# Layer 0 of a two-layer encoder: the dilated heads' queries and keys are projected together for the first four blocks of x, with the loads in that order

## Chip, core and metric

The kernel runs on one core of a Trainium2 chip, in one launch. The metric is the time of one execution on the device in microseconds (us); several runs give a median. One more execution was recorded by the hardware profiler.

The engines are named as in the profile: PE is TensorE, with PEld for the loads of its stationary operand, DVE is VectorE, ACT is ScalarE, POOL is GpSimd and SP is SyncE, which issues most of the loads.

## What is computed

Two layers of an encoder over 256 positions of width 1024, in float32. Each layer has a mixer with three kinds of attention heads, and then a gated feed-forward part with a short convolution. The change is in the first products of the first mixer: `h @ w_in_l`, whose columns hold nine parts, among them `qd` and `kd`, the queries and keys of the six dilated heads, 384 columns each and side by side.

```python
def mixer_sublayer(x, n1, w_in_l, qg, kg, rpb_l, og, w_out_l, tables):
    h = rms_norm(x, n1)
    proj = h @ w_in_l
    sizes = (NA_W, NA_W, NA_W, DIL_W, DIL_W, DIL_W, GQ_W, GKV_W, GKV_W)
    qa, ka, va, qd, kd, vd, qc, kc, vc = jnp.split(proj, cuts, axis=-1)
    ...
    qd = partial_rotary(rms_norm(heads(qd, H_DIL), qg[1]), cos1, sin1)
    kd = partial_rotary(rms_norm(heads(kd, H_DIL), kg[1]), cos1, sin1)
    out_d = dilated_window_attention(qd, kd, heads(vd, H_DIL), dil_idx, dil_val)
    ...
    return x + mix @ w_out_l
```

## The kernel before

**Numbers and products.** Every float32 operand of a product is split into a rounded part (`hi`, a cast on ScalarE) and the rest (`lo`, a subtraction on VectorE), and a product is made of three: hi x hi, hi x lo, lo x hi (`mm3`). x stands in SBUF as two tiles of 128 positions (t = 0, 1). For the products it is turned on TensorE, block by block: 1024 columns are eight blocks of 128 (k = 0 to 7). A block takes two transpositions, then ScalarE scales it by the gains of the norm into `hT_hi` and VectorE makes `hT_lo`. The gains themselves are loaded as rows and turned first (`gains_T`); the division by the root of the mean square comes later, in the heads.

**Units.** The weights come in units of up to 2048 columns per partition, `PROJ` for `w_in`: the first unit is dq (the dilated queries) with blocks 0 to 3, the second dq with blocks 4 to 7, the third and fourth dk in the same way, then dv, cq, ckv, aqk, av. A unit is loaded into one of four `raw` buffers (`load`), split in slices into one of two pairs `hi`, `lo` (`split`), and used (`unit`). In `projections` a unit's products go over t, then over its blocks, so a block of dq with 384 columns is six products: three for each t. Each of dq and dk needs two of the four PSUM banks `psa`; dv takes the banks of dq again, when their values have been scaled and copied out.

**Order.** The kernel is first written down as a list (`Plan.add`), and then ordered by the planner in `Plan.order`, which takes, over all engines, the operation that can start first by its own estimates, and of several the one with the lower rank. A rank is the place in the list, a shift (`later`) and a correction from the table `PLACES`, by number of the operation. `START` is the hand-written order of the first loads, on SP's queue and on ScalarE's, and `LANDS` the times at which the planner expects them. `WARM` products of a constant, 256 columns in bfloat16, run on TensorE before its first data are there; `WARM_MORE` of them fill gaps among the first transpositions.

Almost every operation has the line 520 in the profile (519 after the change), since one helper records them all; so rows are told apart by the names of tiles: `psa` and `psw` are PSUM banks of products and of the rest, `act_hT` the turned x, `wp_raw`, `wp_hi`, `wp_lo` the weights, `const_x` the input, `act_s2k` a work buffer that holds the gains' rows at first.

## Time and profile before

| | us |
|---|---|
| median of 3 runs | 595.01 |
| lowest and highest | 594.70, 595.23 |
| the profiled execution | 595.39 |
| its span, first to last instruction | 593.6 |
| PE busy in the span | 587.5 |
| DVE, ACT busy | 470.2, 412.1 |

A busy TensorE is not the same as one that waits for nothing: products are pipelined, and two that follow each other at once overlap in the rows. So holes are read from the starts of products, and from the waits of the weight loads (PEld), which the trace gives with what ended them.

### The profile page before, as it was taken

How to read it: one execution, taken by the hardware profiler on the slowest of the kernel's cores; microseconds unless marked ns; L12 is line 12 of the kernel's file. 1: busy time of each engine (PE TensorE's matmuls, PEld its weight loads, DVE VectorE, ACT ScalarE, POOL GpSimd, SP SyncE). 2: the span in 40 equal slices, each digit the busy share in tenths (PEclk: the TensorE clock that was granted, in tenths of full speed). 3: DMA queues.
4: the chain of work that ended last, by engine and by line, in shares of the span. 5: the costliest groups of instructions: out<-in, count | busy, mean ns of one | idle time of the engine just before them, and what ended most of it. 6: DMA issues, size and time to landing. Idle time of an engine off the chain costs nothing.

```text
span 593.6 us, 9687 instructions
## 1 busy us (share of the span) xinstructions
PE 587.5 (99%) x3424; PEld 506.9 (85%) x3424; DVE 470.2 (79%) x983; ACT 412.1 (69%) x1035; POOL 78.3 (13%) x126
## 2 busy tenths in 40 slices
PE   9999999999999999999999999999999999999997
PEld 7998887888888888888899988778888888888886
DVE  5799889888779879778787896777876867776596
ACT  7789988676575766756697998476665656564581
POOL 1734121250000000000032225321000000000000
PEclk9999999999999999999999999999999999999999
DMA  8892313565589599899556527943455735666411
GB/s 294 307 323 105 107 36 121 202 213 192 180 245 371 207 342 346 290 318 323 170 153 213 203 73 252 340 142 120 155 201 167 240 118 186 213 215 211 142 71 72
DMA packets 85073, 121.38 MB, mean 204 GB/s; under 512 B 9864, under 2 KB 69736, under 8 KB 85024
## 3 DMA queue, kind: packets, MB, share of 16 engines
q1 hardware_dynamic: 82752, 112.10, 56.5%
q0 software_dynamic: 1728, 8.39, 4.0%
q8 instruction: 27, 0.44, 0.3%
q10 hardware_dynamic: 544, 0.26, 0.1%
q14 instruction: 22, 0.18, 0.1%
HBM read 110.86 MB, written 9.88 MB: 203 GB/s over the span
## 4 chain that ended last, share of the span: by engine, by line
PE 90%; POOL 3%; issue 2%; DMA 2%; DVE 2%; ACT 0%; POOLq 0%; ACTq 0%
PE psw_w L520 50%; PE psa_a L520 40%; POOL small_rstd L520 1%; DMA wp_hi<-dram_khi 1%; POOL small_ms L520 1%; DMA wp_raw<-in_w_in_dram 1%; DVE act_z L520 0%; DVE wp_lo L520 0%; DVE act_s2k L520 0%; POOL act_scq L520 0%; ACT act_s2k L520 0%; DVE act_sw L520 0%; POOL act_sck L520 0%; POOL act_sqm L520 0%; POOL wp_lo L520 0%
## 5 line engine op out<-in xcount | busy, mean ns | idle before, releaser
L520 DVE TENSOR_TENSOR wp_lo<-wp_raw,wp_hi 128x512 fp32r<-128x512 f32 (+2 forms) x332 | 233.7, 733 | 36.6 <-ACT wp_hi L520 22.7
L520 ACT CAST wp_hi<-wp_raw 128x512 fp32r<-128x512 f32 (+2 forms) x332 | 202.4, 665 | 19.9 <-PE psa_a L520 10.1
L520 PE MATMUL psw_w<-act_hT,wp_hi 128*128 128x512 f32 x704 | 177.1, 392 | 0.0
L520 PEld LDWEIGHTS psw_w<-act_hT,wp_hi 128*128 128x128 f32 x704 | 129.0, 188 | 24.8 <-DVE act_hT L520 0.3
L520 PE MATMUL psa_a<-wp_hi,act_hT 128*128 128x384 f32 (+2 forms) x448 | 112.8, 333 | 0.1
L520 PEld LDWEIGHTS psw_w<-act_hT,wp_lo 128*128 128x128 f32 x704 | 94.8, 188 | 6.3
L520 PE MATMUL psw_w<-act_hT,wp_lo 128*128 128x256 f32 x704 | 99.0, 280 | 0.0
L520 PEld LDWEIGHTS psa_a<-wp_hi,act_hT 128*128 128x128 f32 x448 | 77.7, 188 | 3.2 <-ACT act_hT L520 0.3
L520 PE MATMUL psa_a<-wp_lo,act_hT 128*128 128x384 f32 (+2 forms) x224 | 72.8, 331 | 0.5 <-DVE wp_lo L520 0.4
L520 DVE TENSOR_TENSOR act_s2k<-psw_w,act_s2k 128x256 f32<-128x256 f32 x88 | 36.2, 421 | 40.0 <-ACT act_s2k L520 39.6
L520 PE MATMUL psa_a<-wp_lo,act_ch 128*128 128x512 f32 (+1 forms) x176 | 67.6, 388 | 0.0
L520 PE MATMUL psa_a<-wp_hi,act_cl 128*128 128x512 f32 (+1 forms) x176 | 66.3, 388 | 0.0
L520 ACT COPY act_s2k<-psw_w 128x256 f32<-128x256 f32 x88 | 32.1, 372 | 47.1 <-PE psw_w L520 46.9
L520 PE MATMUL psa_a<-wp_hi,act_ch 128*128 128x512 f32 (+1 forms) x176 | 64.6, 388 | 0.0
L520 PEld LDWEIGHTS psa_a<-wp_lo,act_hT 128*128 128x128 f32 x224 | 42.0, 188 | 2.7 <-DVE wp_lo L520 1.4
L520 ACT ACTIVATE act_s2k<-act_s2k,act_cw 128x256 f32<-128x256 f32 x44 | 24.1, 595 | 22.4 <-DVE act_s2k L520 22.4
L520 DVE SCALAR_TENSOR_TENSOR act_s2k<-act_s2k,act_cw,act_s2k 128x255 f32<-128x255 f32 x88 | 37.8, 479 | 1.2 <-ACT act_s2k L520 0.7
L520 PEld LDWEIGHTS psa_a<-wp_hi,act_cl 128*128 128x128 f32 x176 | 33.0, 188 | 6.4
L520 PEld LDWEIGHTS psa_a<-wp_lo,act_ch 128*128 128x128 f32 x176 | 33.1, 188 | 6.2
L520 PEld LDWEIGHTS psa_a<-wp_hi,act_ch 128*128 128x128 f32 x176 | 32.7, 188 | 5.9
L520 POOL TENSOR_TENSOR small_rstd<-small_ms,const_mh 128x6 f32<-128x6 f32 (+2 forms) x26 | 32.6, 1257 | 17.2 <-DVE small_ms L520 15.8
L520 ACT ACTIVATE act_s2k<-act_s2k 128x512 f32<-128x512 f32 x22 | 13.9, 632 | 24.0 <-DVE act_s2k L520 24.0
(131 smaller groups left out, 701.2 us busy)
## 6 DMA issues: line engine op xcount, KB each, us to landing
wp_raw<-in_w_gate_up_dram SPq DMA_DIRECT2D x44, 1024.0 KB, 5.1
wp_raw<-in_w_down_dram SPq DMA_DIRECT2D x22, 1024.0 KB, 5.5
wp_raw<-in_w_in_dram SPq DMA_DIRECT2D x14, 768.0 KB, 6.1
wp_raw<-in_w_in_dram SPq DMA_DIRECT2D x8, 1024.0 KB, 7.6
wp_raw<-in_w_out_dram SPq DMA_DIRECT2D x8, 768.0 KB, 6.6
dram_khi<-act_mixT_hi SPq DMA_DIRECT2D x4, 768.0 KB, 5.6
dram_klo<-act_mixT_lo SPq DMA_DIRECT2D x4, 768.0 KB, 9.1
wp_lo<-dram_klo POOLq DMA_DIRECT2D x4, 768.0 KB, 4.8
```

Source lines behind the costliest of these rows:

```text
L520: getattr(o.engine.real, o.method)(*map(real, o.args), **{k: real(v) for k, v in o.kw.items()})
```

## The change

In layer 0 the first two units are now 768 columns wide, dq and dk side by side, with two blocks of x each: unit 0 has blocks 0 and 1, unit 1 blocks 2 and 3. The third unit is dq with blocks 4 to 7, the fourth dk with blocks 4 to 7 (`proj_of`). `projections` opens all four banks at once and goes over these two units block by block: for each block, dq and dk for both t, twelve products of 384 columns. From the third unit on it is as before, and layer 1 is as before.

The first loads follow that. Unit 0's first block is loaded in two halves by ScalarE's queue, and SP's queue begins with the first block of x and the first gains. The slices in which ScalarE and VectorE split the first two units stay at 384 columns. `WARM` goes from 14 to 12. `LANDS` and the whole of `PLACES` have new numbers, so that every rank in the program can differ.

The lists below stand in program order; names are those of the profile with buffer numbers (`wp_hi0` is the first of two buffers, `psa_a1` a bank), and `x2` means twice in a row.

TensorE, the first real products. Before:

```order
L520 MATMUL psa_a1_143<-wp_hi0_113,act_hT0_135 128x384
L520 MATMUL psa_a1_143<-wp_lo0_119,act_hT0_135 128x384
L520 MATMUL psa_a2_148<-wp_hi0_113,act_hT0_135 128x384
L520 MATMUL psa_a2_148<-wp_lo0_119,act_hT0_135 128x384
L520 MATMUL psa_a1_143<-wp_hi0_113,act_hT0_135 128x384 x2
L520 MATMUL psa_a2_148<-wp_hi0_113,act_hT0_135 128x384 x2
L520 MATMUL psa_a1_143<-wp_lo0_119,act_hT0_135 128x384
L520 MATMUL psw_w3_165<-const_ident0_85,const_x0_79 128x128 x2
L520 MATMUL psw_w0_121<-const_ident0_85,const_x0_79 128x128 x2
L520 MATMUL psa_a1_143<-wp_hi0_113,act_hT0_135 128x384
L520 MATMUL psa_a2_148<-wp_lo0_119,act_hT0_135 128x384
L520 MATMUL psa_a2_148<-wp_hi0_113,act_hT0_135 128x384
```

After:

```order
L519 MATMUL psa_a1_140<-wp_hi0_116,act_hT0_130 128x384
L519 MATMUL psa_a1_140<-wp_lo0_127,act_hT0_130 128x384
L519 MATMUL psa_a1_140<-wp_hi0_116,act_hT0_130 128x384
L519 MATMUL psa_a2_147<-wp_hi0_116,act_hT0_130 128x384
L519 MATMUL psa_a2_147<-wp_lo0_127,act_hT0_130 128x384
L519 MATMUL psa_a2_147<-wp_hi0_116,act_hT0_130 128x384
L519 MATMUL psa_a3_154<-wp_hi0_116,act_hT0_130 128x384
L519 MATMUL psa_a3_154<-wp_lo0_127,act_hT0_130 128x384
L519 MATMUL psa_a3_154<-wp_hi0_116,act_hT0_130 128x384
L519 MATMUL psa_a0_83<-wp_hi0_116,act_hT0_130 128x384
L519 MATMUL psa_a0_83<-wp_lo0_127,act_hT0_130 128x384
L519 MATMUL psa_a0_83<-wp_hi0_116,act_hT0_130 128x384
```

Before, the first block's six products lie in banks 1 and 2 and the next block follows; after, the first block has twelve, in all four banks.

ScalarE, from its first instruction. Before:

```order
L520 DMA const_x0_79<-in_x_dram 128x2x128 x2
L520 ACT_TABLE_LOAD
L520 CAST wp_hi0_113<-wp_raw0_81 128x384
L520 ACTIVATE act_hT0_135<-psw_w1_125,const_gains0_130 128x256
L520 ACTIVATE act_hT0_135<-psw_w2_128,const_gains0_130 128x256
L520 CAST wp_hi0_113<-wp_raw0_81 128x384
L520 ACTIVATE act_s2k2_163,small_ssx0_162<-const_x0_79 128x512
L520 CAST wp_hi0_113<-wp_raw0_81 128x384 x2
L520 ACTIVATE act_hT0_135<-psw_w3_165,const_gains0_130 128x256
L520 ACTIVATE act_hT0_135<-psw_w0_121,const_gains0_130 128x256
L520 ACTIVATE act_s2k3_196,small_ssx0_162<-const_x0_79 128x512
L520 ACTIVATE act_hT0_135<-psw_w1_125,const_gains0_130 128x256 x2
```

After:

```order
L519 DMA wp_raw0_79<-in_w_in_dram 128x384 x2
L519 ACT_TABLE_LOAD
L519 CAST wp_hi0_116<-wp_raw0_79 128x384
L519 ACTIVATE act_hT0_130<-psw_w1_118,const_gains0_123 128x256
L519 CAST wp_hi0_116<-wp_raw0_79 128x384
L519 ACTIVATE act_hT0_130<-psw_w2_125,const_gains0_123 128x256
L519 CAST wp_hi0_116<-wp_raw0_79 128x384 x2
L519 CAST wp_hi1_169<-wp_raw1_105 128x384 x2
L519 ACTIVATE act_s2k2_185,small_ssx0_184<-const_x0_81 128x512
L519 ACTIVATE act_hT0_130<-psw_w3_182,const_gains0_123 128x256
L519 ACTIVATE act_hT0_130<-psw_w0_114,const_gains0_123 128x256
L519 ACTIVATE act_s2k3_205,small_ssx0_184<-const_x0_81 128x512
```

ScalarE issued two loads of x, and now issues two of weights; the first cast still stands ahead of the first two `act_hT`, but another cast now stands between those, and four casts (a block each of units 0 and 1) ahead of the first square of x.

SP, from the last unit of dk on. Before:

```order
L520 DMA wp_raw3_159<-in_w_in_dram 128x4x384
L520 DMA const_rot0_167<-in_c_rot_dram 128x2x208
L520 DMA const_gq0_175<-in_q_norm_g_dram 128x384
L520 DMA const_gk0_179<-in_k_norm_g_dram 128x384
L520 DMA act_few0_185<-in_rpb_dram 28x1x31
L520 DMA const_dil0_193<-in_c_dil_dram 128x2x256
L520 DMA wp_raw0_81<-in_w_in_dram 128x4x384
```

After:

```order
L519 DMA wp_raw3_156<-in_w_in_dram 128x4x384
L519 DMA const_gq0_162<-in_q_norm_g_dram 128x384
L519 DMA act_few0_171<-in_rpb_dram 28x1x31
L519 DMA const_rot0_178<-in_c_rot_dram 128x2x208
L519 DMA wp_raw0_79<-in_w_in_dram 128x4x384
L519 DMA const_gk0_196<-in_k_norm_g_dram 128x384
L519 DMA const_dil0_202<-in_c_dil_dram 128x2x256
```

`wp_raw0` with four blocks of 384 is the load of dv's first half. Before, five small loads stood ahead of it, after, three; the gains of the keys and the dilated bias come behind it. Ahead of what is shown SP has the loads of `START`. On POOL, in layer 1, the loads of the second kept weights (`wp_lo` and `wp_hi` from DRAM), which had an addition between them, now follow each other.

```diff
--- before.py
+++ after.py
@@ -49,16 +49,16 @@
 
 
 START = [
-    ("act", "x", (0, 1)), ("sync", "w", 0), ("act", "x", (1, 1)), ("sync", "g", 0), ("sync", "w", 1),
-    ("sync", "x", (2, 2)), ("sync", "w", 2), ("sync", "w", 3), ("sync", "x", (4, 2)), ("sync", "x", (6, 2)),
-    ("sync", "g", 1), ("sync", "g", 2),
+    ("act", "w", (0, 0, 0, 384)), ("sync", "x", (0, 1)), ("act", "w", (0, 0, 384, 768)), ("sync", "g", 0),
+    ("sync", "x", (1, 1)), ("sync", "w", (0, 1, 0, 768)), ("sync", "w", (1, 0, 0, 768)), ("sync", "x", (2, 2)),
+    ("sync", "w", (1, 1, 0, 768)), ("sync", "x", (4, 2)), ("sync", "x", (6, 2)), ("sync", "g", 1), ("sync", "g", 2),
 ]
 
 
-LANDS = (3600, 3500, 4300, 4100, 5600, 7000, 7200, 7700, 8500, 9300, 9350, 9400)
-
-
-WARM, WARM_MORE, WARM_W = 14, 6, 256
+LANDS = (3600, 3100, 4500, 3400, 4100, 6300, 7100, 7700, 8700, 9400, 10100, 10150, 10200)
+
+
+WARM, WARM_MORE, WARM_W = 12, 6, 256
 
 SUM_ACT, SCALE_ACT = ("dq", "dk", "cq"), ("dk",)
 
@@ -234,45 +234,44 @@
 
 
 PLACES = {
-    76: 315, 114: 87, 123: -69, 140: 162, 157: -5, 158: -5, 159: -5, 162: 341, 171: 193, 202: 194, 213: 279,
...
+    120: -12, 153: -12, 155: -19, 158: 141, 159: -69, 188: -46, 190: -19, 193: -4, 207: 48, 223: -26, 239: -36,
...
 }
@@ -655,12 +654,21 @@
     def rows(w, k0, n, c0, width):
         return w[k0 * P : (k0 + n) * P, c0 : c0 + width].rearrange("(k p) c -> p k c", p=P)
 
+    def proj_of(l):
+
+        parts_ = []
+        for i, (c0, width) in enumerate(PROJ):
+            per = 4 if width * 8 > UNIT else 8
+            parts_ += [(c0, width, k0, per) for k0 in range(0, KD, per)]
+        if l == 0:
+            (c0, width), per = PROJ[0], KD // 4
+            parts_[:4] = [(c0, 2 * width, 0, per), (c0, 2 * width, per, per), parts_[1], parts_[3]]
+        return parts_
+
     def units_of(l):
 
-        for c0, width in PROJ:
-            per = 4 if width * 8 > UNIT else 8
-            for k0 in range(0, KD, per):
-                yield rows(w_in[l], k0, per, c0, width)
+        for c0, width, k0, per in proj_of(l):
+            yield rows(w_in[l], k0, per, c0, width)
         for gi, c0 in OUT_ORDER:
             yield rows(w_out[l], *OUTP[gi], c0, 512)
         for kind, s in FFN:
@@ -707,19 +715,20 @@
         raw = wp.tile([P, UNIT], F32, tag="raw", name=f"raw{i}", bufs=RAWS)
         rv = raw[:, : a * b].rearrange("p (a b) -> p a b", b=b)
         if i == 0:
+            raws.extend([raw, wp.tile([P, UNIT], F32, tag="raw", name="raw1", bufs=RAWS)])
             for by, what, c in START:
                 by = nc.scalar if by == "act" else nc.sync
                 if what == "w":
-                    by.dma_start(rv[:, c], v[:, c])
+                    u, k, e, f = c
+                    to = raws[u][:, : a * b].rearrange("p (a b) -> p a b", b=b)
+                    by.dma_start(to[:, k, e:f], views[u][:, k, e:f])
                 elif what == "x":
                     load_x(*c, by)
                 elif what == "g":
                     by.dma_start(gl0 if c == 0 else gl1[16 * c - 16 : 16 * c], gsrc[c])
             nc.first_loads = len(nc.ops)
-        else:
-            for c in range(0, a, 2 if i == 1 else a):
-                e = c + 2 if i == 1 else a
-                nc.sync.dma_start(rv[:, c:e], v[:, c:e])
+            return
+        nc.sync.dma_start(rv, v)
         raws.append(raw)
 
     def split(i):
@@ -735,7 +744,7 @@
         j = i % PER_LAYER - LAST_OUT
         here, low = (0, ASIDE if j >= 0 and FFN[j][0] != "D" else 0) if j >= 0 or b != S else (EVEN - ASIDE,) * 2
         hi, lo = hi[:, here : here + UNIT], lo[:, low : low + UNIT]
-        h = b if i < 2 else b * max(1, CHUNK // b)
+        h = PROJ[0][1] if i < 2 else b * max(1, CHUNK // b)
         if i in kept:
             for d, z in zip(kept[i], (hi, lo)):
                 nc.gpsimd.dma_start(z[:, :n], d)
@@ -952,19 +961,32 @@
         pj = {}
 
         def projections():
-            for (c0, width), name in zip(PROJ, PROJ_NAMES):
-                ps = [psa.tile([P, 512], F32, tag="a", name=f"pj_{name}{l}{t}") for t in range(NT)]
-                per = 4 if width * 8 > UNIT else 8
-                for k0 in range(0, KD, per):
+            banks = lambda name: [psa.tile([P, 512], F32, tag="a", name=f"pj_{name}{l}{t}") for t in range(NT)]
+
+            def product(ps, t, kk, wh, wl):
+                c = slice(t * P, (t + 1) * P)
+                mm3(ps[t][:, : wh.shape[1]], hT_hi[:, kk, c], hT_lo[:, kk, c], wh, wl, kk == 0, kk == KD - 1)
+
+            units, width = iter(proj_of(l)), PROJ[0][1]
+            if l == 0:
+                both = [banks(name) for name in PROJ_NAMES[:2]]
+                for _, _, k0, per in (next(units), next(units)):
+                    wh, wl = unit()
+                    for k in range(per):
+                        for i, ps in enumerate(both):
+                            cs = slice(i * width, (i + 1) * width)
+                            for t in range(NT):
+                                product(ps, t, k0 + k, wh[:, k, cs], wl[:, k, cs])
+                                yield 3 * width / 2.4
+            for n, ((c0, width), name) in enumerate(zip(PROJ, PROJ_NAMES)):
+                ps = both[n] if l == 0 and n < 2 else banks(name)
+                k0 = per = 0
+                while k0 + per < KD:
+                    _, _, k0, per = next(units)
                     wh, wl = unit()
                     for t in range(NT):
-                        c = slice(t * P, (t + 1) * P)
                         for k in range(per):
-                            kk = k0 + k
-                            mm3(
-                                ps[t][:, :width], hT_hi[:, kk, c], hT_lo[:, kk, c],
-                                wh[:, k], wl[:, k], kk == 0, kk == KD - 1,
-                            )
+                            product(ps, t, k0 + k, wh[:, k], wl[:, k])
                             yield 3 * width / 2.4
                 pj[name] = ps
                 yield name
```

## Rows read from the trace of the kernel before

**Rows 1.** The page, part 1: busy us, share of the span, instructions.

```profile
PE 587.5 (99%) x3424; PEld 506.9 (85%) x3424; DVE 470.2 (79%) x983; ACT 412.1 (69%) x1035; POOL 78.3 (13%) x126
```

**Rows 2.** Stretches: start:end us, length; busy us (count) by engine; granted clock; DMA.

```profile
12.50:20.00 7.50, 7.50 (x43) 7.50 (x44) 5.31 (x10) 6.05 (x35) 3.18 (x7) 1.00 0.91 309
...
50.00:75.00 25.00, 24.57 (x176) 19.37 (x174) 22.44 (x76) 24.34 (x72) 6.35 (x8) 1.00 0.29 96
```

**Rows 3.** Timeline, all engines, to 6 us: start, us, engine, operation [idle before].

```profile
0.99 3.55 PE L520 MATMUL psa_a<-const_warm 128*128 128x256 bf16 x17 [0.99 <-POOL const_warm L520]
...
3.87 0.51 ACT L520 CAST wp_hi<-wp_raw 128x384 fp32r<-128x384 f32 x1 [0.85 <-DMA wp_raw<-in_w_in_dram]
...
4.41 0.56 DVE L520 TENSOR_TENSOR wp_lo<-wp_raw,wp_hi 128x384 fp32r<-128x384 f32 x1 [4.41 <-ACT wp_hi L520]
...
4.51 0.20 PE L520 MATMUL psw_w<-const_ident,act_s2k 16*128 16x16 f32 x1
...
4.65 0.66 PE L520 MATMUL psw_w<-const_ident,const_x 128*128 128x128 f32 x4
4.89 0.17 DVE L520 COPY const_gains<-psw_w 128x16 f32<-128x16 f32 x1
...
5.16 0.84 ACT L520 ACTIVATE act_hT<-psw_w,const_gains 128x256 fp32r<-128x256 f32 x2 [0.78 <-PE psw_w L520]
...
5.68 0.44 PE L520 MATMUL psa_a<-wp_hi,act_hT 128*128 128x384 f32 x1
```

**Rows 4.** Timeline, TensorE alone, 4.4 to 5.8 us: warm-up products.

```profile
4.16 0.38 PE L520 MATMUL psa_a<-const_warm 128*128 128x256 bf16 x2
...
5.14 0.49 PE L520 MATMUL psa_a<-const_warm 128*128 128x256 bf16 x3
```

**Rows 5.** Timeline: one group of four transpositions and the products behind it.

```profile
8.37 0.63 PE L520 MATMUL psw_w<-const_ident,const_x 128*128 128x128 f32 x4
...
9.01 0.34 PE L520 MATMUL psa_a<-wp_lo,act_hT 128*128 128x384 f32 x1
```

**Rows 6.** Timeline of TensorE's weight loads (PEld): the longest waits, with their releasers.

```profile
12.45 0.19 PEld L520 LDWEIGHTS psa_a<-wp_lo,act_hT 128*128 128x128 f32 x1 [0.39 <-DVE wp_lo L520]
...
25.22 0.19 PEld L520 LDWEIGHTS psa_a<-wp_lo,act_hT 128*128 128x128 f32 x1 [0.34 <-DVE wp_lo L520]
...
56.74 0.19 PEld L520 LDWEIGHTS psa_a<-wp_lo,act_hT 128*128 128x128 f32 x1 [0.66 <-DVE wp_lo L520]
...
377.81 0.19 PEld L520 LDWEIGHTS psa_a<-wp_hi,act_mixT_hi 128*128 128x128 f32 x1 [1.19 <-DMA wp_hi<-dram_khi]
```

**Rows 7.** Stretches of the first loads; the last number is GB/s.

```profile
1.50:5.50 4.00, 4.00 (x24) 2.76 (x22) 0.64 (x2) 2.14 (x3) 0.02 (x1) 1.00 0.82 200
2.50:4.25 1.75, 1.75 (x10) 1.25 (x9) 0.00 (x0) 0.90 (x2) 0.00 (x0) 1.00 0.99 296
4.25:5.50 1.25, 1.25 (x11) 0.82 (x9) 0.64 (x2) 0.47 (x2) 0.00 (x0) 1.00 0.65 167
5.50:7.00 1.50, 1.45 (x9) 1.30 (x8) 1.34 (x3) 1.25 (x4) 0.00 (x0) 1.00 1.02 365
15.60:17.40 1.80, 1.80 (x12) 1.80 (x11) 1.20 (x3) 0.39 (x1) 0.46 (x2) 1.00 0.54 122
```

**Rows 8.** Timeline, ScalarE: the square that waited for x, the casts of dv.

```profile
6.72 0.63 ACT L520 ACTIVATE act_s2k<-const_x 128x512 f32<-128x512 f32 x1 [0.25 <-DMA const_x<-in_x_dram]
...
22.06 1.76 ACT L520 CAST wp_hi<-wp_raw 128x384 fp32r<-128x384 f32 x4 [0.82 <-DMA wp_raw<-in_w_in_dram]
```

**Rows 9.** Timeline, ScalarE: hT and casts in a run.

```profile
9.51 1.19 ACT L520 ACTIVATE act_hT<-psw_w,const_gains 128x256 fp32r<-128x256 f32 x3
...
11.19 1.76 ACT L520 CAST wp_hi<-wp_raw 128x384 fp32r<-128x384 f32 x4
```

**Rows 10.** Timeline, POOL: the second kept weights of layer 1.

```profile
369.34 0.64 POOL L520 DMA_DIRECT2D wp_lo<-dram_klo  x1 [0.44 <-PE psa_a L520]
...
370.71 0.57 POOL L520 DMA_DIRECT2D wp_hi<-dram_khi  x1
```

75 rows, old and new, of the table PLACES are left out of this document.

## Prediction

> **What bounds the kernel now.** I read the page first, then the stretches, then the first 25 us engine by engine, then the waits of the weight loads. TensorE is busy for 587.5 of 593.6 us [rows 1], and this is work, not waiting: between 12.5 and 20 us it ran 43 products of 384 columns in 7.50 us, 0.174 us each, with no hole [rows 2]. Its work is fixed, so only three things can move the end: the moment of the first real product, the small holes between products, and what a new order adds. In one stretch a second engine is nearly full: ScalarE, 24.34 of 25 us from 50 to 75 us [rows 2].
>
> The first product starts at 5.68 [rows 3]. Read the chain backwards: ScalarE makes the first block of hT at 5.16; it waited for the gains, which VectorE copied at 4.89, behind its first wp_lo (4.41); TensorE had turned the gains at 4.51, when their load was in. Until 4.51 TensorE only runs warm-up products.
>
> Then the holes. From 5.68 to 12.45 the order of before holds 26 products and 13 transpositions: 26 x 0.174 + 13 x 0.11 = 5.95 us of work in 6.77, so 0.8 us was lost, 0.39 of it in one wait for wp_lo at 12.45 [rows 6]. The next holes are 0.34 at 25.22 (wp_lo again), 0.66 at 56.74 and 1.19 at 377.81 (the first kept wp_hi, from DRAM) [rows 6]. Seen this way the whole kernel has some 3 to 4 us that an order can win.
>
> **The change part by part.**
> *Work.* TensorE runs the same real products and transpositions; only two warm-up products fewer (18 for 20), which run before the first product and so are paid for in the next term. ScalarE and VectorE split the same weights, in slices of the same 384 columns (four in 1.76 us, one 0.51, so 0.42 from start to start [rows 9]).
>
> *The start.* In the new order 14 warm-up products stand ahead of the gains. Before, 15 took from 0.99 to 4.16 [rows 3, 4], 0.211 each, so 14 end at 3.95: TensorE can take the gains 0.55 us earlier, if they are there; their load and the first block of x now lead SP's queue. VectorE copies the gains ahead of wp_lo, not behind it. But ScalarE now casts the first weights before it makes hT, and these come through ScalarE's own queue. Bounds for their landing: 3.87, where the cast began when they led SP's queue, and 4.65, by which the x block that led ScalarE's queue had landed, since TensorE turned it then [rows 3]. A landing at L gives cast (0.51), hT (0.52 to the product, 5.16 to 5.68) and 0.03 between: first product at L + 1.06, but not under 3.95 + 1.17 = 5.12, the old way from the gains to the product. That is 5.12 to 5.71, or -0.55 to +0.03. I take the middle, L = 4.26: 5.32, **-0.4** in round numbers.
>
> *Block 1's weights.* Block 0 now holds 12 products (2.1 us), so TensorE wants block 1 at 5.32 + 0.1 for the first product after a change + 12 x 0.174 = 7.5. Bytes ahead of and with its 393 KB: 131 + 8 + 131 + 393 on SP, 393 on ScalarE's queue, 1.06 MB. The table [rows 7] gives 200 GB/s over the 4 us to 5.5, 0.80 MB, then 365 GB/s: 1.06 MB at 6.2. To land takes longer: ScalarE's first square waited for x up to 6.72 [rows 8], whose bytes (0.93 MB and some 0.06 of program loads) were through at about 6.0, so 0.7 later. Block 1 lands near 6.9, its first wp_hi is ready at 7.45 and its first wp_lo at 8.05, against 7.9 wanted by the third of its products: a wait of about **+0.2**; 0 if it lands 0.3 earlier, 0.6 if 0.4 later. The Trainium skill (Trainium Kernel Development and Optimization, Key Constraints) says that loads issued from several engines run on the same 16 DMA engines, so that only issue time is saved. The table half agrees: 296 GB/s with both queues, 167 when SP's was left alone at 4.25 to 5.5, but 365 with SP alone a moment later; by that rule block 1 lands as worked out, and with the slow stretch filled it would land some 0.2 us earlier.
>
> *The hole at 12 us.* The same 26 products and 13 transpositions now leave the third unit until both heads' first four blocks are done. ScalarE has, from 6.9 on, six casts (0.42), four squares (0.63 [rows 8]) and six pieces of hT (0.36: three in 1.19 [rows 9], two in 0.84 [rows 3]): 7.1 us, so it begins the third unit at about 14.0 and the first wp_lo is there at 15.1. TensorE comes to it at 5.32 + 0.1 + 48 x 0.174 + 13 x 0.11 + 0.3 for changes of kind + 0.2 of wait = 15.7. The cover is half a microsecond; so the hole goes, though not the changes between products and transpositions: **-0.4**, from 0 (the cover is gone) to -0.7.
>
> *The hole at 25 us.* It stands behind dv's weights: they were cast at 22.06, when they had landed [rows 8]; in SP's order there stood ahead of them the rotation table, both gains, the rows of rpb and the dilated bias, and the queue moved only 122 GB/s from 15.6 to 17.4 [rows 7]. Now gk and the bias (458 KB, 1.25 us at 365 GB/s) stand behind them, while TensorE wants them no earlier: **-0.35**, from 0 to -0.5.
>
> *More changes of kind.* In the new order TensorE goes from products to transpositions 65 times for 56 and back 70 for 59. Four transpositions with the product behind them took 0.64 us, 8.37 to 9.01 [rows 5]; less the product that leaves 0.47, or 0.03 over 4 x 0.11. Ten more such groups: **+0.2**, bounds 0 to 0.7.
>
> *The kept weights.* Before, wp_lo went out on POOL at 369.34, an addition came between, and wp_hi followed at 370.71 [rows 10]; TensorE waited 1.19 for this wp_hi [rows 6]. Now both go out back to back, some 0.7 us earlier. Other loads share the engines after that, so I take less than half: **-0.3**, from -1.0 to +0.3.
>
> *Elsewhere.* All ranks are new. The heads' first products come at the same place in TensorE's work (within 0.5 us), so the q bank freed later (72 products instead of 48) should not show: dv wants it 24 products, 4.2 us, after the last of dq; between stand six small squares, the reciprocal root on POOL and one scaled copy, and of the two banks the one wanted first is done 12 products earlier. The new order's own waits can't be seen from the old trace. The old ones at 56.74 (0.66) and 25.22 show their size: I put **+0.25**, from -0.7 to +1.5.
>
> Sum: -0.4 + 0.2 - 0.4 - 0.35 + 0.2 - 0.3 + 0.25 = -0.8. The profiled execution took 595.39 (span 593.6 and 1.8 around it); the change acts inside the span, 595.39 to 594.6. The median of the runs, 595.01, lies 0.38 lower, so the forecast for a median is **594.2**.
>
> **Rivals.**
> *The gains all come.* Weights at 3.87, block 1 in time, holes at 12 and 25 us gone whole, wp_hi 0.7 earlier: -0.55 + 0 - 0.7 - 0.5 + 0.2 - 0.7 + 0.25 = -2.0, **593.0**; half of that surplus already passes 0.2%. For it speaks that the holes are single waits with one cause each; against it, that the first weights would have to come as early from a queue that has shown only x.
> *Block 1 starves TensorE.* The slow stretch of the loads (167 GB/s) with more bytes behind it: 0.6 at block 1 and as much at its transpositions of x, nothing won at the start: 0 + 1.2 - 0.4 - 0.35 + 0.2 - 0.3 + 0.25 = +0.6, **595.6**, no change.
> *A late clock.* Before, warm-up products started 0.211 us apart until 4.16 and 0.11 apart from then on (three in 0.49, two in 0.38 [rows 4]): 256 columns in those times are the 1.2 and the 2.4 GHz level, though the table's granted clock says 1.00 [rows 7]; TensorE had worked without a hole since 0.99. The new order has 14 products, then the gains and x with a possible hole, and real products 0.4 earlier. If the rise comes only after block 0, its 12 products take twice 0.174: +2.1, **596.3**, slower. It decides at the hole before the gains: none, and the rise comes as before. The Trainium skill (TensorE: Matmul & The Clock Gate, Parts 1 and 4) says that the slow state is the default, released by activity, and that transpositions don't count as busy in the same way; by it the earlier and mixed start could cost this 2.1. The trace shows two levels but no late rise.
> *New waits in the attention.* Where ScalarE is 97% busy [rows 2], work put off to that stretch comes out at the end one for one; 2.5 us of it on top gives **596.7**.
>
> **How the numbers follow.** What a measurement can tell from no change is about 0.2%, 1.19 us: 593.82 to 596.2. Forecast case (593.82 to 594.9): 0.44. All gains: 0.34. Starved block: 0.09. Late clock: 0.07. New waits: 0.06. So faster 0.34, same 0.44 + 0.09 = 0.53, slower 0.13. The range leaves out the two slow cases and the far end of the gains: 592.7 to 595.6.
>
> **What the profile after would show.** Start right: first product of hT between 5.1 and 5.4, warm-ups of 0.11 before it. Block 1: a wait of at most 0.3 for wp_hi or wp_lo near 7.5 to 8. Holes: no wait over 0.2 for wp_lo between 10 and 28 us. Kept weights: the wait for wp_hi in layer 1 under 0.9. Transpositions: total of TensorE's idle no larger. It is wrong if the first product stands at 5.6 or later, if products of block 0 start 0.35 apart, or if the time won by 30 us is given back by 115 us, where the first gate product shows it.

## The result and the profile after

The kernel after takes 598.02 us at the median of 8 executions (596.15 to 598.47), the kernel before 595.12 us (594.41 to 596.45): a ratio of 1.0039, with a 95% interval of 1.0023 to 1.0054. It is slower, by more than 0.2%, and outside the range given. The 8 times stand in two groups with nothing between them: 596.15, 596.38 and 596.49, and five from 597.96 to 598.47. The profiled execution (596.49, span 594.6) is of the lower group, so its trace explains about 1 us of the loss, and another 1.9 us (between the medians of the two groups) in more than half of the executions has to be found elsewhere.

The page of the kernel after, part 1, to set beside [rows 1]:

```profile
PE 588.0 (99%) x3422; PEld 507.4 (85%) x3422; DVE 472.9 (80%) x983; ACT 410.7 (69%) x1035; POOL 80.7 (14%) x126
```

TensorE's work is the same; the span grew by what it waits. Where, is read by matching work: for each product, the sum of the work ahead of it on TensorE is the same quantity in both kernels, so the starts at equal work can be subtracted. This table is worked out from all product starts of the traces (work in us of product time, warm-up products left out; with another way of counting the work an entry moves by up to 0.1). The last two columns are differences to before, of the runs e9 and e10 below:

| work done | before at | after at | difference | run e9 | run e10 |
|---|---|---|---|---|---|
| 2 | 7.33 | 7.83 | +0.50 | +0.40 | +0.96 |
| 8 | 14.17 | 13.98 | -0.19 | -0.05 | +0.16 |
| 15 | 21.14 | 21.29 | +0.15 | +0.29 | +0.50 |
| 25 | 31.95 | 31.33 | -0.62 | -0.49 | -0.28 |
| 40 | 46.20 | 45.78 | -0.43 | -0.27 | -0.06 |
| 45 | 51.21 | 51.64 | +0.44 | -0.28 | -0.07 |
| 120 | 127.11 | 128.18 | +1.07 | -0.26 | -0.06 |
| 340 | 347.21 | 349.06 | +1.85 | -0.26 | -0.03 |
| 360 | 367.01 | 368.54 | +1.53 | -0.59 | -0.36 |
| 370 | 378.07 | 378.84 | +0.77 | -0.77 | -1.37 |
| last product | 589.73 | 590.68 | +0.95 | +0.14 | -1.38 |

So the start lost half a microsecond, the holes at 12 and 25 us were won, and from 45 us on more was lost than the kept weights at 370 gave back.

**The start.** Timeline of TensorE and of ScalarE in the kernel after, to set beside [rows 3]:

```profile
0.98 3.17 PE L519 MATMUL psa_a<-const_warm 128*128 128x256 bf16 x14 [0.98 <-POOL const_warm L519]
4.37 0.26 PE L519 MATMUL psw_w<-const_ident,act_s2k 16*128 16x16 f32 x1 [0.22 <-DMA act_s2k<-in_norm_g_dram]
4.56 0.69 PE L519 MATMUL psw_w<-const_ident,const_x 128*128 128x128 f32 x2
5.04 0.33 PE L519 MATMUL psa_a<-const_warm 128*128 128x256 bf16 x1
5.70 0.44 PE L519 MATMUL psw_w<-const_ident,const_x 128*128 128x128 f32 x2 [0.33 <-DMA const_x<-in_x_dram]
5.98 0.49 PE L519 MATMUL psa_a<-const_warm 128*128 128x256 bf16 x3
6.22 0.42 PE L519 MATMUL psa_a<-wp_hi,act_hT 128*128 128x384 f32 x1
...
3.63 0.51 ACT L519 CAST wp_hi<-wp_raw 128x384 fp32r<-128x384 f32 x1 [0.68 <-DMA wp_raw<-in_w_in_dram]
5.28 0.47 ACT L519 ACTIVATE act_hT<-psw_w,const_gains 128x256 fp32r<-128x256 f32 x1 [1.14 <-PE psw_w L519]
```

The weights from ScalarE's queue were early (3.63, before 3.87). The gains, second on SP's queue, were turned at 4.37 (4.51 before), not at 3.95, and hT was made at 5.28, not at 4.8: two transpositions of x took 0.69 us ahead of it, where before four took 0.66 [rows 3]. Then TensorE's own order cost more: ahead of the first product stand the transpositions of the second block of x, which TensorE waited for until 5.70, and four warm-up products. The first product of hT starts at 6.22, 0.54 later than before; in six more profiles of the kernel after at 6.04 to 6.34. In those six TensorE turns the second block earlier, at 5.25 to 5.44; there its transpositions and the warm-up products follow each other 0.213 us apart, the 1.2 GHz level, until 5.9 or later.

**The longest waits.** PEld in the kernel after, those of about 0.35 us and more that the kernel before doesn't have at this work, to set beside [rows 6]:

```profile
50.33 0.14 PEld L519 LDWEIGHTS psw_w<-const_ident,act_s2k 128*128 128x128 f32 x1 [1.01 <-ACT act_s2k L519]
...
116.00 0.19 PEld L519 LDWEIGHTS psw_w<-act_hT,wp_hi 128*128 128x128 f32 x1 [0.60 <-DVE act_hT L519]
...
322.70 0.19 PEld L519 LDWEIGHTS psa_a<-wp_lo,act_hT 128*128 128x128 f32 x1 [0.35 <-DVE wp_lo L519]
...
378.61 0.42 PEld L519 LDWEIGHTS psw_w<-const_ident,act_s2k 128*128 128x128 f32 x4 [0.61 <-ACT act_s2k L519]
```

No wait for wp_lo between 10 and 28 us is left, nor one for the kept wp_hi in layer 1 (0.39, 0.34 and 1.19 us before); the 0.61 at 378.61 stands near its place. New is 1.01 us at 50.33: a softmax of the dilated heads, not ready when TensorE wants to turn it. Its origin stands on VectorE, 5 us earlier, first in the kernel before, then in the one after:

```profile
44.83 0.42 DVE L520 CUSTOM_DVE_ANT_0 act_s2k<-psw_w,const_dil 128x256 f32<-128x256 f32 x1
...
46.13 0.56 DVE L520 TENSOR_TENSOR act_z<-psa_a,small_rstd 128x384 f32<-128x384 f32 x1 [0.53 <-POOL small_rstd L520]
```

```profile
45.38 0.56 DVE L519 TENSOR_TENSOR act_z<-psa_a,small_rstd 128x384 f32<-128x384 f32 x1 [1.58 <-POOL small_rstd L519]
45.85 0.41 DVE L519 CUSTOM_DVE_ANT_0 act_s2k<-psw_w,const_dil 128x256 f32<-128x256 f32 x1
```

`act_z` scales the compressed queries by a reciprocal root that POOL makes. Before, the masked row maxima of the first dilated head (the custom instruction) went first; after, they queue behind `act_z`, and VectorE stands 1.58 us, most of it with them ready (in e4 below they start at 44.15).

### The profile page after: what moved, and what is told of

Read it like the earlier page. It is cut to its first block, busy times and chain, and to the rows that moved or that the text cites. A ratio compares the mean times of both kernels' runs of the same rounds, so it can differ in the third digit from the quotient of the medians.

```text
span 594.6 us, 9687 instructions
## 1 busy us (share of the span) xinstructions
PE 588.0 (99%) x3422; PEld 507.4 (85%) x3422; DVE 472.9 (80%) x983; ACT 410.7 (69%) x1035; POOL 80.7 (14%) x126
## 4 chain that ended last, share of the span: by engine, by line
PE 88%; DVE 5%; ACT 3%; issue 2%; POOL 2%; DMA 1%; SPq 0%; DVEq 0%; POOLq 0%
PE psw_w L519 49%; PE psa_a L519 39%; ACT act_s2k L519 2%; DVE wp_lo L519 2%; POOL small_rstd L519 1%; DVE act_z L519 1%; DMA const_x<-in_x_dram 1%; DVE small_nm L519 1%; DVE const_x L519 1%; POOL small_ms L519 0%; DVE act_s2k L519 0%; ACT wp_hi L519 0%; DVE act_sw L519 0%; DVE small_ss L519 0%; ACT act_z L519 0%
## 5 line engine op out<-in xcount | busy, mean ns | idle before, releaser
L519 PE MATMUL psw_w<-act_hT,wp_lo 128*128 128x256 f32 x704 | 100.5, 279 | 0.0
L519 PE MATMUL psa_a<-wp_lo,act_hT 128*128 128x384 f32 (+2 forms) x224 | 74.0, 334 | 0.0
```

The lines of the kernel that those rows point to most:

```text
L519: getattr(o.engine.real, o.method)(*map(real, o.args), **{k: real(v) for k, v in o.kw.items()})
```

## Experiments

An order is changed in what follows after the planner has made it: MOVED takes an instruction (by its number) and puts it ahead of another in the list, TIMES says how often one is issued. All else is then where it was.

**e1: the holes ahead of the first product filled.**

```diff
+TIMES = {16: 4, 17: 6}   # warm-up products: the last ahead of the gains, the one between the x blocks
-                getattr(o.engine.real, o.method)(...)
+                for _ in range(TIMES.get(i, 1)):
+                    getattr(o.engine.real, o.method)(...)
```

> The kernel after, whose TensorE stands idle from 3.95 to 4.37 us and from 5.25 to 5.70 us; here three more warm-up products stand ahead of the gains and five more between the first and the second block of x, so that TensorE has no hole before the first real product; nothing else is moved. Theory: the executions of after fall into two groups, 596.15 to 596.5 and 598.0 to 598.5, because the clock of TensorE rises before or after the first twelve products, and the holes decide that. Then all executions here are in the lower group, median 596.0 to 596.5, and the warm-up products change from 0.213 to 0.11 us apart near 4.2 us, as in the kernel before. Rival: the upper group comes from something else (landings of loads, say); then two groups remain and the median stays at 598. First real product at 6.2 to 6.3 by both.

Median 596.56 of 11, 596.15 to 597.34; ratio to before 1.0022 (1.0013 to 1.0031). None of the 11 is in the upper group. But on the same chip the unfilled start gave only one such execution in 15 (11 of e4, four of the kernel after itself under e13), so this run doesn't tell the theory from its rival. The first product came at 6.43. In its profile the clock did not rise at 4.2 but at 5.2, as the spacing of the warm-up products shows (17 took 3.8 us, six then 0.82 with their tail).

**e2: holes in the kernel before.** Five warm-up products left out, TIMES = {18: 0, 19: 0, 20: 0, 21: 0, 22: 0}.

> The kernel before without five of its warm-up products, the last two ahead of the gains and the three behind the first transpositions, so that TensorE is idle from about 4.0 to 4.5 us and from 5.1 to 5.7 us, much as in the kernel after; nothing else is moved. Theory (holes before the first product make the clock rise later): some or most executions 1.5 to 2.1 us longer than before, so 596.6 to 597.2, and in a profile of such a one the first products 0.35 us apart. Rival (holes there do no harm): 595.1, as before, and the first product at 5.68.

Median 595.29 (ratio 1.0004, 0.9994 to 1.0013), but two groups: six of 11 at 594.84 to 595.29, five at 596.33 to 597.18. The profile (596.45) is of the upper one. The stretch from 6 to 8 us, first of before, then of after, of e2 and of e17 (below); the count behind PE is the reading:

```profile
6.00:8.00 2.00, 2.00 (x14) 1.87 (x13) 1.19 (x4) 1.75 (x5) 0.00 (x0) 1.00 1.07 384
```

```profile
6.00:8.00 2.00, 2.00 (x15) 1.98 (x13) 1.66 (x5) 1.56 (x4) 0.00 (x0) 1.00 0.93 285
```

```profile
6.00:8.00 2.00, 2.00 (x7) 2.00 (x8) 1.13 (x3) 1.18 (x5) 0.00 (x0) 1.00 1.04 366
```

```profile
6.00:8.00 2.00, 2.00 (x7) 1.98 (x8) 1.20 (x3) 0.95 (x3) 0.00 (x0) 1.00 0.95 333
```

Seven instead of 14 or 15 in the same 2 us: in e2 products start 0.32 apart up to 8.8 us, which is 384 columns at the 1.2 GHz level; the granted clock in the row reads 1.00 all the same. So holes at the start can leave TensorE at the lower level into its first products, and not in every execution.

**e3: the first loads in the order of before.**

```diff
 START = [
-    ("act", "w", (0, 0, 0, 384)), ("sync", "x", (0, 1)), ("act", "w", (0, 0, 384, 768)), ("sync", "g", 0),
-    ("sync", "x", (1, 1)), ("sync", "w", (0, 1, 0, 768)), ...
+    ("act", "x", (0, 1)), ("sync", "w", (0, 0, 0, 384)), ("act", "x", (1, 1)), ("sync", "g", 0),
+    ("sync", "w", (0, 0, 384, 768)), ("sync", "w", (0, 1, 0, 768)), ...
```

> The kernel after with the first loads in the order and on the queues of the kernel before: the first two blocks of x on ScalarE's queue, the two halves of the first weights on SP's. No other instruction is moved. Theory (after starts late, at 6.22 instead of 5.68, because the gains landed at 4.37 and the second block of x only at 5.70, behind 786 KB of other loads, and the first product stands behind that block's transpositions in TensorE's order): first product at 5.6 to 5.8, lower group 595.8 (596.35 less 0.5). Rival (the order on the queues doesn't matter, since all loads share their engines): first product at 6.1 or later and 596.3. If the hole from 5.25 to 5.70 is what makes the upper group, that group is gone and the median is 595.8; if it is the hole at 3.95, it stays and the median is 597.5.

Median 596.66 (ratio 1.0027, 1.0016 to 1.0037): nothing won. The profile (598.07) shows why. First TensorE, then PEld, in two stretches:

```profile
5.55 0.44 PE L519 MATMUL psa_a<-wp_hi,act_hT 128*128 128x384 f32 x1
```

```profile
10.05 0.42 PEld L519 LDWEIGHTS psw_w<-const_ident,const_x 128*128 128x128 f32 x4 [1.13 <-DMA const_x<-in_x_dram]
...
396.09 0.19 PEld L519 LDWEIGHTS psa_a<-wp_hi,act_mixT_hi 128*128 128x128 f32 x1 [0.93 <-DMA wp_hi<-dram_khi]
```

The first product came 0.67 earlier than in after, and then TensorE stood 1.13 us for the third block of x: the half microsecond was taken back within 4.5 us. This is the slowest of the seven executions, and no other has a trace. Its 598.07 is not a late clock (from the fourth on, its first products stand 0.174 apart); it is these two waits for loads.

**e4: the row maxima ahead of the scaling.** In the kernel after, MOVED = [(513, 466), (512, 466)].

> The kernel after with two instructions moved on VectorE: the two masked row maxima of the first dilated head go ahead of the scaling of the compressed queries, which in the profile after waits 1.58 us (43.8 to 45.4 us) for the reciprocal root on POOL with these two queued behind it. Theory (this wait is passed on by way of ScalarE's softmax to TensorE, which stands 0.86 us at 49.25): that wait falls below 0.2 and the time by 0.6 to 0.9, lower group 595.5. Rival (ScalarE, 100% busy from 50 to 62 us, is the bound, so the wait comes back at one of the next transpositions): less than 0.3 won. The two groups of executions stay by both, since the start is untouched.

Median 595.83 (ratio 1.0011, 1.0002 to 1.0020); ten of 11 at 595.62 to 596.08, so about 0.5 below after's lower group, and one at 598.06. VectorE and PEld of e4:

```profile
44.15 0.42 DVE L526 CUSTOM_DVE_ANT_0 act_s2k<-psw_w,const_dil 128x256 f32<-128x256 f32 x1 [0.41 <-PE psw_w L526]
...
45.32 0.56 DVE L526 TENSOR_TENSOR act_z<-psa_a,small_rstd 128x384 f32<-128x384 f32 x1 [0.40 <-POOL small_rstd L526]
```

```profile
49.85 0.14 PEld L526 LDWEIGHTS psw_w<-const_ident,act_s2k 128*128 128x128 f32 x1 [0.59 <-ACT act_s2k L526]
```

The wait on VectorE fell from 1.58 to 0.40 with nothing ready behind it, and PEld's fell from 1.01 to 0.59, not below 0.2: ScalarE then waits 1.17 us for the reciprocals of the row sums, which still stand behind in VectorE's order. The mechanism holds, and most of the price: 0.5 of the 0.6 to 0.9. ScalarE as the bound would have left less than 0.3.

**e5, e11, e13: the kernel after again,** unchanged, for its two groups.

> The kernel after, unchanged, beside its variants on one chip, since with the same start one variant had only 1 of 11 executions in the upper group where after had 5 of 8. Theory (the upper group is a late rise of TensorE's clock, which depends on where the start falls against something the program doesn't set): two groups again, near 596.3 and 598.1, in another proportion; if the profile is one of the upper group, its first nine products stand 0.32 us apart. Rival (the upper group is a wait somewhere else): in a profile of the upper group the first products stand 0.174 us apart and a wait of over 1 us shows later.

> The kernel after, unchanged, for one more profile: one in two or three is of the upper group. Theory (late clock): if the time is 597.9 or more, nine or more of the first products stand 0.32 us apart and the rest is as in the other profiles. Rival (a wait elsewhere): products 0.174 apart from the start, and a wait of about 1.5 us at another place.

> The kernel after, unchanged, for one more profile. If it is above 597.5 us: late clock, then nine or more first products 0.32 us apart; late loads, then products 0.174 us apart from the start and waits of over 0.6 us at 8 to 9 us or at 380 to 396 us. If it is below 597: as the three profiles so far.

e5: median 596.91 of 12 (ratio 1.0025, 1.0015 to 1.0035): eight from 596.26 to 597.13, four from 597.91 to 599.36. e11 gave 596.55, e13 596.35, and three more with the words of e13 596.24, 596.55 and 596.55. All these profiles are of the lower group, so an upper execution of the kernel after itself has not been seen in a trace.

**e6, e12, e18: more holes in the kernel after.** TIMES = {15: 0, 16: 0, 17: 0, 18: 0, 19: 0, 20: 0}: six warm-up products left out.

> The kernel after without its last two warm-up products ahead of the gains and the four around the second block of x: TensorE is idle from 3.5 to 4.4 us and nearly so from 5.1 to 6.2; nothing else is moved. Theory (holes before the first product put off the rise of the clock): more executions in the upper group than of after on the same chip, at least half, median 597.5 to 598.3, and first products 0.32 us apart in a profile of such a one. Rival (the upper group has another cause): the same proportion as after, first products 0.174 us apart.

> The kernel after without six warm-up products, as once before, for one more profile: half of its executions stand above 597.2. Theory (late clock): if the time is 597.2 or more, first products 0.32 us apart. Rival (a wait elsewhere, for instance for the first loads): products 0.174 apart and a wait of over 1 us.

> The kernel after without six warm-up products, one more profile. Above 597.2: late clock if the first products stand 0.32 us apart, late loads if they stand 0.174 apart and a wait of over 0.8 us shows at 8 to 9 or at 380 to 396 us. Below 597: as its two profiles so far.

e6: median 597.38 (ratio 1.0029, 1.0018 to 1.0039), 595.98 to 599.42, six of 12 above 597.5, where e5 on the same chip had four of 12: too near to tell the theory from its rival. e12 gave 596.45 and e18 596.27; so all three profiles are again of lower executions, and from the fourth on their first products stand 0.174 apart. They show one thing more. TensorE of e6:

```profile
4.43 0.20 PE L523 MATMUL psw_w<-const_ident,act_s2k 16*128 16x16 f32 x1 [0.70 <-DMA act_s2k<-in_norm_g_dram]
4.56 0.78 PE L523 MATMUL psw_w<-const_ident,const_x 128*128 128x128 f32 x4
5.56 0.44 PE L523 MATMUL psa_a<-wp_hi,act_hT 128*128 128x384 f32 x1 [0.22 <-ACT act_hT L523]
```

Without the four warm-up products around the second block of x, and with that block there in time, the first product starts at 5.56, 0.66 earlier than in after's profile; in e12 and e18 at 5.60 and 5.59. But TensorE stands at the upper level here from the gains on (0.13 us from the gains to x, as in before, against 0.19 in after), in spite of the larger hole. So some of after's late start is its own filling at the lower level; how much is the filling and how much the level, no run separates.

**e17: a late clock on purpose.** The kernel after with six warm-up products instead of eighteen, TIMES = 0 for 9 to 20.

> The kernel after with six warm-up products instead of eighteen, all at the start: TensorE is idle from 2.3 us to the gains at 4.4; nothing else is moved. Theory (the upper group of after is a late clock): nearly all executions above 597.5, median 598.0 to 598.5 like that group, and in the profile nine or more first products 0.32 us apart. Rival (the upper group is late loads): the clock is late here too, if it can be, but the time is another, 597.3 or less, or two groups remain.

Median 598.31 (ratio 1.0043, 1.0029 to 1.0056), all six from 597.42 to 599.0. Its profile (597.42, the lowest) has eight products at the lower level, 0.32 apart, the last row of the four above. Where the clock is made late, the times fall where after's upper group lies; that a time lies there doesn't yet tell its cause (e3).

**e7: the load of dv earlier, in the kernel before.** MOVED = [(159, 296), (295, 296)]: the keys' gains and the dilated bias go behind it.

> The kernel before with the loads of the keys' gains and of the dilated bias behind the first load of dv instead of ahead of it; nothing else is moved. Theory (the hole of 0.34 and 0.4 us near 24 to 25 us in the kernel before comes from dv's load, which landed at 22.06 behind these): the wait for wp_lo near 25 us falls below 0.15, dv's casts begin at 21.2 or earlier, and the time falls by 0.3, to 595.0 or less, if nothing later takes it back. Rival (the heads, whose tables come later now, or ScalarE from 50 us on take it back): the hole is gone but the time stays at 595.3.

Median 595.59 (ratio 1.0000, 0.9992 to 1.0009): nothing won. The load did come earlier: ScalarE waited for it until 22.06 before [rows 8], and here it had landed at 19.4, so that the casts run on without a wait. But TensorE's wait for wp_lo is still there, at the same product, now at 26.07 since the program stands 0.85 us later; its 0.19 lies above the 0.15 expected. It is as long in e8 below, where dv's load is not moved. PEld of e7, then of e8:

```profile
26.07 0.19 PEld L527 LDWEIGHTS psa_a<-wp_lo,act_hT 128*128 128x128 f32 x1 [0.19 <-DVE wp_lo L527]
```

```profile
25.08 0.19 PEld L527 LDWEIGHTS psa_a<-wp_lo,act_hT 128*128 128x128 f32 x1 [0.19 <-DVE wp_lo L527]
```

By equal work e7 wins 0.32 on before's profile here (+1.17 at 15 us of work, +0.85 at 20), and so do e8 (+0.18, -0.15) and e2 (+1.96, +1.60) without the move. So the hole is not dv's load. Where it comes from stands on VectorE, first before, then e7:

```profile
23.55 0.56 DVE L520 TENSOR_TENSOR act_z<-psa_a,small_rstd 128x384 f32<-128x384 f32 x1 [1.61 <-POOL small_rstd L520]
...
24.61 0.55 DVE L520 TENSOR_TENSOR wp_lo<-wp_raw,wp_hi 128x384 fp32r<-128x384 f32 x1
```

```profile
24.41 0.56 DVE L527 TENSOR_TENSOR act_z<-psa_a,small_rstd 128x384 f32<-128x384 f32 x1 [1.25 <-POOL small_rstd L527]
...
25.47 0.55 DVE L527 TENSOR_TENSOR wp_lo<-wp_raw,wp_hi 128x384 fp32r<-128x384 f32 x1
```

The wp_lo that TensorE waits for is made behind `act_z`, the scaling of dq, and that waits for POOL's reciprocal root: 1.61 us in before's profile, 1.24 to 1.25 in e2, e7 and e8. It is the mechanism seen at 45 us in the kernel after. There, at this place, it is gone: POOL makes the root right behind its mean square, and `act_z` doesn't wait. POOL and VectorE of the kernel after:

```profile
21.05 1.66 POOL L519 TENSOR_TENSOR small_rstd<-small_ms,const_mh 128x6 f32<-128x6 f32 x1
...
23.13 0.55 DVE L519 TENSOR_TENSOR act_z<-psa_a,small_rstd 128x384 f32<-128x384 f32 x1
```

The profile of e7 shows one thing more: before's own start, unchanged, with the first product at 6.27 instead of 5.68. TensorE of e7, to set beside [rows 3]:

```profile
4.94 1.11 PE L527 MATMUL psw_w<-const_ident,const_x 128*128 128x128 f32 x4
5.84 0.67 PE L527 MATMUL psa_a<-const_warm 128*128 128x256 bf16 x3
6.27 0.42 PE L527 MATMUL psa_a<-wp_hi,act_hT 128*128 128x384 f32 x1
```

Four transpositions take 1.11 us instead of 0.66: all twenty warm-up products were there, and the lower level lasted until 6.2 all the same.

**e8: the kept loads next to each other, in the kernel before.** MOVED = [(3831, 3581)].

> The kernel before with one instruction moved on POOL: the addition between the two loads of the second kept weights goes behind them, so that the load of wp_hi is issued at 370.0 instead of 370.7 us. Theory (TensorE's wait of 1.19 us at 377.8 ends with this load): the wait falls to 0.4 to 0.6 and the time by 0.5. Rival (the load is held up by the others that share its engines, and its landing hardly moves; or the wait is passed on to the next kept weights): less than 0.2.

Median 594.94 (ratio 0.9990, 0.9981 to 0.9998), faster than before. POOL and TensorE:

```profile
369.18 0.64 POOL L527 DMA_DIRECT2D wp_lo<-dram_klo  x1 [0.44 <-PE psa_a L527]
369.82 0.54 POOL L527 DMA_DIRECT2D wp_hi<-dram_khi  x1
370.36 0.75 POOL L527 TENSOR_TENSOR act_sqm<-act_sqm,act_sqm 128x256 f32<-128x256 f32 x1
```

```profile
376.49 0.39 PE L527 MATMUL psa_a<-wp_hi,act_mixT_lo 128*128 128x512 f32 x1
376.72 0.39 PE L527 MATMUL psa_a<-wp_hi,act_mixT_hi 128*128 128x512 f32 x1
```

The second is the product that waited for the kept wp_hi at 377.81 [rows 6]; its wait of 1.19 us is gone, by equal work 1.0 us.

**e9: the kernel after to 44 us, then the order of before.** The planner's search is replaced by a table: after's own first 421 instructions, and then before's order of the rest, instruction by instruction.

```diff
+ORDER = [
...
+]
-            best = None
-            for e, r in ready.items():
...
-            at, _, i = best
+            i = ORDER[len(done)]
+            at = at_of(ops[i])
```

> The kernel after up to about 44 us (its loads, its 768-wide units, its order of the first 421 instructions), and from there on every engine in the order of the kernel before. Theory (what after loses behind 45 us comes from the new ranks, not from the wider units): at 45 us it stands 0.4 us ahead of before, as after does in its profile, and keeps that, since the waits at 49 us (0.86), 115 us (0.33) and 322 us (0.2) are not in this order; after's loss of 1.4 us from there to the end is gone, lower group 595.0. Rival (the wider units bring the heads' inputs at other times, so the order of before waits too): lower group 596.0 or more. The upper group stays in some of the executions by both.

Median 594.79 (ratio 0.9992, 0.9982 to 1.0002), six from 593.88 to 594.79 and five from 595.46 to 596.66. The column in the table above says the rest: the lead it has at 40 us of work stays to the hundredth up to 340, where after lost 2.3 us (-0.43 to +1.85). So the 768-wide units cost nothing behind 44 us; the new ranks do. Its profile (595.64) is of the upper five, and its clock is not late; what it loses at the end are kept weights, late again (PEld):

```profile
377.04 0.19 PEld L800 LDWEIGHTS psa_a<-wp_hi,act_mixT_hi 128*128 128x128 f32 x1 [1.04 <-DMA wp_hi<-dram_khi]
...
389.03 0.19 PEld L800 LDWEIGHTS psa_a<-wp_lo,act_mixT_hi 128*128 128x128 f32 x1 [1.04 <-DMA wp_lo<-dram_klo]
```

**e10: e9, with the filling of e1 and the kept loads of e8.**

> As the run before it, with two more edits that earlier runs showed: the warm-up products that fill the holes at the start, and the two loads of the second kept weights of layer 1 next to each other on POOL. Theory (the terms add up): 595.0 less 0.7 for the kept weights, and no upper group: median 594.2 to 594.6, below before. Rival (the terms overlap, since a wait that ends with a load takes in what is won ahead of it): 594.9, as the kernel before with the kept loads together.

Median 594.15 of 8, 593.55 to 594.64; ratio 0.9975 (0.9965 to 0.9986): faster than both kernels, without an upper group, and the kept weights aren't waited for. It has the wider units of the change, so these were not what made the kernel slower. Most of what it wins on before is the kept loads: e8 has them alone and stands at -1.21 at the last product, e10 at -1.38.

## Why the prediction was wrong

The forecast was 594.2. The lower group stands 2.2 above it: the start missed 0.9 and the new order behind 40 us 2.0, while the kept weights, block 1 and the changes of kind came out 0.9 better than counted. The upper group stands 1.9 higher still.

**The start** was the first step that failed: -0.4 forecast, +0.54 measured, beyond its bound of +0.03. The chain chosen was landing of the weights, cast, hT, and the weights came earlier than the chosen 4.26. What the chain left out is TensorE's own order: the transpositions of the second block of x and four warm-up products stand ahead of the first product. In six profiles TensorE ran through them at the lower level; in two (after's first, e9's) it waited for the block until 5.6 to 5.7; of all executions with this start the earliest first product came at 5.89 (e4). And the gains, taken to be there at 3.95, were turned at 4.37. The level itself has a share that stays open: with before's own start and a late rise the first product came at 6.27 (e7). The rule of the Trainium skill (Trainium Kernel Development and Optimization, Key Constraints) that loads from several engines share the 16 DMA engines was weighed for block 1 only; e3's one profile agrees with it for the whole start: another distribution over the queues moved a wait from 5.7 to 10 us, and the runs won nothing.

**The late clock** was a rival with the right size: 2.1 forecast, 12 x (0.320 - 0.174) = 1.75 with the spacing of e2 and e17, and 1.9 between the medians of after's groups. Its chance of 0.07 rested on the gains being there at 3.95. It failed also in form: it was taken as a case, yes or no, and it comes in some executions and not in others. What is shown: holes bring such a group into the kernel before, with the late clock in its trace (e2), and a clock late on purpose puts after's times there (e17). Against the hole as the switch stand e6, e12 and e18, with larger holes and an early rise, and e7, with none and a late one. With the holes filled none of 19 executions was in the group (e1, e10), without 9 of 25 of the kernel after; but these counts come from several chips, and on e1's own it was one of 15. That after's upper executions are late clocks is thus likely from the size, but not shown, since none of them has a trace; in e3 and e9 it is late loads that make an execution long.

**Elsewhere** was put at +0.25 with a bound of +1.5; from 40 to 340 us of work it was +2.28. The mechanism was named (an order's own waits in the attention) but looked for on ScalarE, at 97%. The largest piece, 0.87 by 45 us of work, was VectorE, waiting for POOL with ready work behind; e4 returns 0.5 of it. The other 1.4 is spread over waits such as those at 116.00 and 322.70 and was not taken apart; e9 returns all.

**The hole at 12 us** was right: -0.4 forecast, -0.45 measured (+0.58 at 5 us of work to +0.13 at 10). **The hole at 25 us** went as forecast, with the wrong cause: not dv's load but VectorE's wait for POOL (e7), which the new order took away. That the -0.35 came true was luck, and half of the 0.34 belongs to that one profile, since the wait is 0.17 to 0.19 in e2 and e8. **The kept weights** had the right cause and were worth two to three times the -0.3: -0.76 in after, -1.0 in e8's profile. **Block 1's weights** landed as worked out (cast from 6.97, its first wp_lo made by 8.05), and cost nothing for the 0.2, since TensorE came to them 0.9 us later than forecast: from 6.49 to 8.93 its products start 0.174 apart on average. **More changes of kind** cost next to nothing: in after four transpositions between two products take from 10.73 to the product at 11.26 and on to 11.52, 0.79 us, where their own times (two products of 0.174, four of 0.109) make 0.78. The 0.03 of the forecast stands in that one group; the next one in before, 9.19 to 9.98, took 0.79 too.

Of the marks given ahead, two came true against the forecast: the first product behind 5.6, and the time won by 30 us (-0.62 at 25 us of work) given back by 115 (+1.07 at 120).

## To carry to other kernels

Cost an earlier start by all the operands that the first product needs and by everything that stands ahead of it on its own queue, filling included. When a table of ranks is replaced along with a structure, take them apart: here the structure cost nothing (0.27 us ahead at 40 us in e9) and the new order behind it did, and one run that joined the two orders said so. An engine that waits with ready work queued behind it is to be looked for on the engines that look free, too. And before a hole that is gone is put down to an edit, look whether it is also gone in profiles without the edit.

## What was not expected of the hardware

TensorE's level at the start is not the same in every execution of one program, and the profile's granted clock read 1.00 in all of them, so only the spacing tells (0.213 and 0.11 us for the warm-up products, 0.32 and 0.174 for products of 384 columns). With the start of before it rose at 3.9 us (e8), 4.2 (before) and 6.2 (e7); with the start of after between 5.0 and 6.7 in eight profiles and by 4.5 in one (e9); with after's start and larger holes by 4.5 in all three (e6, e12, e18), and at 8.6 with the largest (e17); in e2 only behind 8.8. So neither a hole ahead of the first product nor its filling settles the moment alone. With the same first loads as before, the first product came at 5.47 in e8, 5.68 in before and 6.27 in e7, in the order of these rises; such a difference between executions hides a gain of 0.3 us.
